# All gate chunks by seven block products, and the retention's heads moved beside the branch products

## The chip, the core and the metric

The kernel runs on one core of a Trainium2 chip. The core has a matrix engine (TensorE, PE in the rows), whose weight loads are shown apart (PEld), an elementwise engine (VectorE, DVE), an engine for activation functions (ScalarE, ACT), a general one (GpSimd, POOL) and SyncE (SP), which here only issues DMAs. Sixteen DMA engines serve them all. The metric is the device time of one launch in microseconds (us).

## The reference

One encoder layer on 256 tokens of width 2048, in float32. Cut to what matters here:

```
h = rmsnorm(x);  proj = h @ w_in            # neighbourhood q,k,v | retention q,k,v,gate | cross-attention q | 3 gates
o_na  = neighbourhood_attention(...)        # 8 heads of 128
o_ret = head_group_norm(retention(fwd) + retention(bwd)) * silu(rg)      # 8 heads, v of 256 a head
o_mem = cross_attention(..., rmsnorm(mem) @ w_mem_kv)                    # 4 heads of 256
merged = sigmoid(g_na) * (o_na @ w_br_na) + sigmoid(g_mem) * (o_mem @ w_br_mem) + sigmoid(g_ret) * (o_ret @ w_br_ret)
x = x + merged @ w_out
x = x + square(relu(rmsnorm(x) @ w_ff1)) @ w_ff2
```

## The kernel before

**Three matmuls for one product.** Every float32 operand is split into a high and a low part: ACT copies the high part (`w_hi`, L95), DVE subtracts it to get the low one (`w_lo`, L96). A product is then hi*hi, lo*hi and hi*lo, three matmuls in `mm3` (L102 to L104).

**Units.** The program is a list of units, which TensorE works through in order. A plain unit multiplies two blocks of 128 rows of a weight (one tile of 512 KB, 128x1024) for both halves of the tokens into 512 columns: 12 matmuls. Eight such units make a chunk of 512 columns of `w_in`; a chunk of `w_br_na` or `w_br_mem` has four. A unit's weights are loaded four units ahead (`issue`, queue SP, five `raw` buffers) and split two units ahead (`do_split`, four buffers each of `w_hi` and `w_lo`).

**Seven block products.** `seven` computes two chunks at once by a scheme of Strassen's kind: 7 instead of 8 block products, each in four units of 6 matmuls (`Product`), so 28 units and 168 matmuls for two chunks where the plain way takes 192. It needs sums of weight blocks. `b1` and `b2` are rings of two buffers each: `ring_load` loads a block into one by SP, `ring_add` adds another block onto it in the DMA itself, issued by POOL (L666), and `do` adds one tile to another on DVE (L682) before the split. A unit's actions have leads: (8, ...) runs eight units ahead of the product, `LEAD` is 14, `L_SPLIT` is 3. For one k the units stand in the order m3, m5, m7 of k-1, m6, m2, m4. In m5 `b1` is the sum of two blocks; in m6 `b1` gets `b2` added on DVE, after which `b2` gets another block added by DMA for m7.

**Order of the stages.** Attention and cross-attention first; then half of the retention's projections; then five pairs of gate chunks by `seven`, with the other 80 plain units of the retention's projections spread between their 140 units; then the last two gate chunks, plainly (`gate_plain`, 16 units); then the branch products with `w_br_na` (16 units), `w_br_mem` (16) and `w_br_ret` (32), whose results are multiplied by the fetched gates on DVE and summed into `merged` (L930, L933, L934); then `w_out`; then the feed-forward layer, whose first product again runs by `seven` in seven pairs (`ff1_pair`) with the plain units of the second product between.

**Tasks.** Smaller work stands in generators that `run_tasks` steps after each unit, at most two steps a unit, at most one that wants the PSUM pool `pt` and one that wants `ps`. `ret_group` fetches what two retention heads need (spilled to DRAM earlier), computes their decay factors, transposes q and k, and spawns the two heads (`ret_head`) and the next group. A head has a chain of products, splits, statistics, a power on POOL (`rsqrt_mean`, L168) and transposes (L554). A scheduler then sorts each engine's instructions by when it holds them to be ready, so the final order is not that of the code.

Of the kernel before, what the change touches and what calls it, by code (L numbers as in the profile page):

```python
# [12 lines left out]
F32 = mybir.dt.float32  # L13
# [44 lines left out]
def encoder_layer(ctx: ExitStack, tc: tile.TileContext, a, out):  # L58
# [259 lines left out]
    def new_T(name):  # L318
        return [quad(f"{name}_{x}") for x in ("hi", "lo")]
# [147 lines left out]
    def decay_factors(g):  # L467

        lg, Fd, V = na_env["lg"], na_env["Fd"], nc.vector
        e1, e2 = cst["dist_f"], cst["dist_b"]  # L470
        Fq = quad("Fd", F32).rearrange("p a s -> p (a s)")
        for h in (2 * g, 2 * g + 1):
            t = t2f("junk")[:, :3 * P]
            Fd[h] = Fq[:, (h % 2) * 3 * P:(h % 2 + 1) * 3 * P]
            V.tensor_scalar_mul(t, e1, lg[:, h:h + 1])
            V.scalar_tensor_tensor(t, e2, lg[:, RET_H + h:RET_H + h + 1], t, op0=ALU.mult, op1=ALU.add)
            nc.scalar.activation(t, t, AF.Exp)
            V.tensor_scalar_mul(Fd[h], t, RET_QK ** -0.5)
# [23 lines left out]
    def ret_group(g):  # L502

        q2 = by_tok(fetch(ret_dram["q", g], "ret_q"))
        v = [by_tok(fetch(d, f"ret_v_{x}", F32R)) for d, x in zip(ret_dram["v", g], ("hi", "lo"))]
        gs = by_tok(fetch(ret_dram["g", g], "ret_gs"))
        yield None, 4
        decay_factors(g)
        T = new_T("ret_qkT")
        for t in range(NT):  # L510
            yield "pt", 1
            pt = transposes(q2[:, t, :], range(4))
            split(T[0][:, :, t * P:(t + 1) * P], T[1][:, :, t * P:(t + 1) * P], pt)
        for j in range(2):
            spawn(ret_head(2 * g + j, j, T, v, gs, env["oT_ret"]))
        if g + 1 < 4:
            spawn(ret_group(g + 1))

    def ret_head(h, j, qkT, v, gs, oT):
        Fd = na_env["Fd"]  # L520
# [137 lines left out]
    def seven(w1, w2, left, halves, r, finish, out_units):  # L658


        V = nc.vector
        e = {}
        NK = 4

        def land(t, src, eng=nc.sync, **kw):
            eng.dma_start(t.rearrange("p (b c) -> p b c", b=2) if len(src.shape) == 3 else t, src, **kw)  # L666

        def raw_load(key, src):
            e[key] = wp.tile([P, UK * CW], F32, name="raw", bufs=5)
            land(e[key], src)  # L670

        def ring_load(n, k, src):
            if not ring:
                open_rings()
            land(ring[n][k % 2], src)

        def ring_add(n, k, src):
            land(ring[n][k % 2], src, nc.gpsimd, accum_op=ALU.add)

        def do(key, raw, add=None):  # L680
            if add is not None:
                V.tensor_tensor(raw, raw, add, op=ALU.add)  # L682
            e[key] = split_w(raw)

        def product(b, form, k, hl, start, stop):
            hi, lo = (by_k(t, halves) for t in hl)
            for j in range(UK):
                mm3(bank[b].rearrange("p (b c) -> p b c", b=2), *left(form, UK * k + j), hi[:, j], lo[:, j],
                    start and j == 0, stop and j == UK - 1)

        def plus(o, b, x, t):

            if r is None:
                V.tensor_tensor(o, bank[b], x, op=ALU.add)
            else:
                V.scalar_tensor_tensor(o, bank[b], r[:, t:t + 1], x, op0=ALU.mult, op1=ALU.add)

        def m1(k):
            def mm():
                if not bank:  # L700
                    open_banks()
                product("X", "A11", k, e.pop(("s1", k)), k == 0, k == NK - 1)
                if k == NK - 1:
                    e["m1"] = t2f("m1")
                    nc.scalar.activation(e["m1"], bank["X"], AF.Copy, **({} if r is None else {"scale": r[:, 0:1]}))
            return Product(mm, [(L_LOAD, lambda: raw_load(("r1", k), w1[k])),
                                (L_SPLIT, lambda: do(("s1", k), e.pop(("r1", k))))])

        def m2(k):
            def mm():  # L710
                product("X", "A12", k, e.pop(("s2", k)), k == 0, k == NK - 1)
                if k == NK - 1:
                    e["c11"] = e["m1"]
                    plus(e["c11"], "X", e["m1"], 0)
            return Product(mm, [(L_LOAD, lambda: raw_load(("r21", k), w1[NK + k])),
                                (L_SPLIT, lambda: do(("s2", k), e[("r21", k)]))])

        def m3(k):
            def mm():
                product("M3", "S4", k, e.pop(("s3", k)), k == 0, k == NK - 1)  # L720
            return Product(mm, [(8, lambda: ring_load("b2", k, w2[NK + k])),
                                (L_SPLIT, lambda: do(("s3", k), ring["b2"][k % 2]))])

        def m5(k):
            def mm():
                product("M5", "S1", k, e.pop(("s5", k)), k == 0, k == NK - 1)
            return Product(mm, [(LEAD, lambda: ring_load("b1", k, w1[k])),
                                (LEAD - 3, lambda: ring_add("b1", k, w2[k])),
                                (L_SPLIT, lambda: do(("s5", k), ring["b1"][k % 2]))])

        def m6(k):
            def pre():
                do(("s6", k), ring["b1"][k % 2], ring["b2"][k % 2])
                ring_add("b2", k, w2[k])

            def mm():
                product("M6", "S2", k, e.pop(("s6", k)), k == 0, k == NK - 1)
                if k == NK - 1:
                    e["u2"] = t2f("u2")
                    V.tensor_tensor(e["u2"], bank["M6"], e["m1"], op=ALU.subtract)  # L740
                    e["c12"] = t2f("c12")
                    V.tensor_tensor(e["c12"], bank["M5"], e["u2"], op=ALU.add)
                    V.tensor_tensor(e["c12"], bank["M3"], e["c12"], op=ALU.add)
            return Product(mm, [(L_SPLIT, pre)])

        def m4(k):
            def mm():
                product("M4", "A22", k, e.pop(("s4", k)), k == 0, k == NK - 1)
            return Product(mm, [(L_SPLIT, lambda: do(("s4", k), ring["b1"][k % 2], e.pop(("r21", k))))])

        def m7(k):
            def mm():
                product("M7", "S3", k, e.pop(("s7", k)), k == 0, k == NK - 1)
                if k == NK - 1:
                    u3 = e["u2"]
                    V.tensor_tensor(u3, u3, bank["M7"], op=ALU.subtract)
                    e["c22"] = t2f("c22")
                    V.tensor_tensor(e["c22"], bank["M5"], u3, op=ALU.add)
                    plus(u3, "M4", u3, 1)
                    e["c21"] = u3  # L760
                    spawn(finish(e))
            return Product(mm, [(L_SPLIT, lambda: do(("s7", k), ring["b2"][k % 2]))])

        out_units += [m1(k) for k in range(NK)]
        for k in range(NK):
            out_units += [m3(k), m5(k)] + ([m7(k - 1)] if k else []) + [m6(k), m2(k), m4(k)]
        out_units.append(m7(NK - 1))
# [56 lines left out]

    gate_dram = {}

    def put_gate(key, sg):
        yield None, 2
        gate_dram[key] = spill(sg, "sg")

    def gate_pair(key, c, ci, to):
        def finish(e):
            sgs = [quad("sg", F32) for _ in range(2)]
# [6 lines left out]
                gate_dram[key, c + i] = spill(sgs[i], f"sg_{key}{c + i}")  # L840

        seven(win(ci), win(ci + 1), x_left, False, r_x, finish, to)

    def gate_plain(key, c, ci):
        def done_gate(acc):
            sg = quad("sg", F32)
            for t in range(NT):
                nc.scalar.activation(by_tok(sg)[:, t, :], acc[t], AF.Sigmoid, scale=r_x[:, t:t + 1])
            spawn(put_gate((key, c), sg))

        chunk(win(ci), hT, KT, done_gate)

    def ret_chunks(g, to):
        def put(key, ts, x=""):
# [39 lines left out]
    ret = ret[16:]  # L894
    sv = []
    for key, c, ci in (("w_br_na", 0, 8), ("w_br_na", 2, 10), ("w_br_mem", 0, 12), ("w_br_mem", 2, 14),
                       ("w_br_ret", 0, 28)):
        gate_pair(key, c, ci, sv)
    n = len(ret)
    for i, x in enumerate(sv):  # L900
# [6 lines left out]
        bank.clear()  # L907

    at(len(units) + 1, end_of_seven)
    at(len(units) + 3, lambda: spawn(ret_group(0)))  # L910
    for i in range(2):
        gate_plain("w_br_ret", 2 + i, 30 + i)


    def branch(wname, oT_key, nkt, first, last):
        at(len(units) - 8, lambda: env[oT_key].back()) if oT_key != "oT_ret" else None
        for c in range(4):
# [25 lines left out]
            at(len(units) - 1, fetch_gate)  # L943
            chunk(w_chunk(wname, c), env[oT_key], nkt, done_br)

    branch("w_br_na", "oT_na", 8, True, False)
    branch("w_br_mem", "oT_mem", 8, False, False)
    branch("w_br_ret", "oT_ret", 16, False, True)
# [145 lines left out]
    for i in range(n_units):  # L1094
# [19 lines left out]
            fn()  # L1114
        do_mm(i)
        units_done.append(i)
        run_tasks(i)
    i = n_units
    while tasks:
        run_tasks(i)  # L1120
# [103 lines left out]
```

## Time and profile before

| | |
|---|---|
| median of 3 runs | 1803.22 us (1802.79 to 1804.96) |
| the profiled execution | 1802.82 us |
| its span in the profile | 1801.1 us |
| TensorE (PE) busy | 1777.3 us, 99% |
| weight loads (PEld) busy | 1467.2 us, 81% |
| DVE busy | 1407.4 us, 78% |
| ACT busy | 1046.3 us, 58% |
| granted TensorE clock | 0.999 of full |

The span runs from the first to the last instruction of the profiled execution; 1.7 us of its time lie outside. Busy time is the union of an engine's instructions. A matmul's end is modelled and overlaps the next one's start, so a busy TensorE can still have lost time: the distance from start to start tells more. Idle time of an engine counts only where TensorE waits for it.

### The profile page before, as it was taken

Reading aid. Unit: us, or ns where it says so; the run is one execution under the profiler, and the core shown is the slowest. Engines: PE = TensorE matmul, PEld = TensorE weight load, DVE = VectorE, ACT = ScalarE, POOL = GpSimd, SP = SyncE. Lnnn points to the kernel's source line nnn. Section 1 sums busy time; section 2 is a strip of 40 time slices with the busy share of each in tenths; the row PEclk is TensorE's granted clock in tenths of the full one; section 3 lists DMA queues with packets and bytes.
Section 4 is the critical chain, followed back from the end, with each engine's and each line's share of the span. In section 5 each row is a group of like instructions: output and inputs, shape, how many; then the busy total and the mean of one; then the engine's idle time right before and its main releaser. Section 6 shows DMA issues by size and latency. Waiting matters only on the chain.

```text
span 1801.1 us, 22755 instructions
## 1 busy us (share of the span) xinstructions
PE 1777.3 (99%) x8130; PEld 1467.2 (81%) x8130; DVE 1407.4 (78%) x1793; ACT 1046.3 (58%) x1313; POOL 148.7 (8%) x176
## 2 busy tenths in 40 slices
PE   8999999999999999999999999998999999999999
PEld 7888888888878888887888888776888888888877
DVE  6777766979888888858875556787898988888874
ACT  7665554656565666654434446855565656666552
POOL 0101000000001000101010000010111111010100
PEclk9999999999999999999999999999999999999999
DMA  9756555899898999987676555787889898979864
GB/s 331 270 204 227 187 175 200 269 300 301 274 302 244 309 289 292 309 303 282 230 255 210 184 185 181 226 237 225 242 254 268 235 270 241 261 227 281 222 187 141
DMA packets 148867, 442.62 MB, mean 246 GB/s; under 512 B 14097, under 2 KB 14609, under 8 KB 148753
## 3 DMA queue, kind: packets, MB, share of 16 engines
q1 hardware_dynamic: 123952, 377.54, 59.3%
q0 software_dynamic: 24512, 62.92, 18.2%
q8 instruction: 64, 1.05, 0.2%
q10 hardware_dynamic: 288, 0.70, 0.1%
q14 instruction: 51, 0.41, 0.1%
HBM read 420.13 MB, written 20.97 MB: 245 GB/s over the span
## 4 chain that ended last, share of the span: by engine, by line
PE 83%; DVE 6%; DMA 5%; ACT 2%; issue 2%; POOL 0%; SPq 0%; DVEq 0%; ACTq 0%; POOLq 0%
PE acc L102 22%; PE acc L103 22%; PE acc L104 22%; PE ps L103 4%; PE ps L104 3%; PE ps L102 3%; DVE w_lo L96 3%; DMA b<-in_w_ff 3%; PE pt L102 2%; PE pt L104 2%; PE pt L103 2%; DMA b<-in_w_in 2%; ACT w_hi L95 1%; DVE b L682 1%; PE pt L315 1%
## 5 line engine op out<-in xcount | busy, mean ns | idle before, releaser
L96 DVE TENSOR_TENSOR w_lo<-raw,w_hi 128x1024 fp32r<-128x1024 f32 (+1 forms) x545 | 660.7, 1220 | 200.1 <-ACT w_hi L95 194.6
L95 ACT ACTIVATE w_hi<-raw 128x1024 fp32r<-128x1024 f32 (+1 forms) x545 | 573.3, 1056 | 372.0 <-PE acc L104 289.0
L95 ACT ACTIVATE w_hi<-b 128x1024 fp32r<-128x1024 f32 x240 | 251.8, 1058 | 258.3 <-PE acc L104 115.7
L96 DVE TENSOR_TENSOR w_lo<-b,w_hi 128x1024 fp32r<-128x1024 f32 x240 | 291.3, 1223 | 112.1 <-ACT w_hi L95 110.1
L102 PE MATMUL acc<-w_hi,hT_hi 128*128 128x512 f32 x744 | 292.2, 393 | 5.7 <-ACT hT_hi L98 5.1
L103 PE MATMUL acc<-w_lo,hT_hi 128*128 128x512 f32 x744 | 291.4, 392 | 0.1
L104 PE MATMUL acc<-w_hi,hT_lo 128*128 128x512 f32 x744 | 290.5, 391 | 0.0
L102 PE MATMUL acc<-w_hi,fT_hi 128*128 128x512 f32 x512 | 201.0, 393 | 2.3 <-DVE x L1046 1.8
L103 PE MATMUL acc<-w_lo,fT_hi 128*128 128x512 f32 x512 | 200.2, 391 | 2.4 <-DVE w_lo L96 2.3
L104 PE MATMUL acc<-w_hi,fT_lo 128*128 128x512 f32 x512 | 199.8, 390 | 0.0
L102 PEld LDWEIGHTS acc<-w_hi,hT_hi 128*128 128x128 f32 x744 | 140.3, 189 | 34.7 <-ACT hT_hi L98 5.1
L103 PEld LDWEIGHTS acc<-w_lo,hT_hi 128*128 128x128 f32 x744 | 140.3, 189 | 30.2 <-DVE w_lo L96 2.5
L104 PEld LDWEIGHTS acc<-w_hi,hT_lo 128*128 128x128 f32 x744 | 140.2, 188 | 29.4
L103 PEld LDWEIGHTS acc<-w_lo,fT_hi 128*128 128x128 f32 x512 | 96.4, 188 | 23.8 <-DVE w_lo L96 4.1
L102 PEld LDWEIGHTS acc<-w_hi,fT_hi 128*128 128x128 f32 x512 | 96.5, 189 | 23.2 <-ACT m L1056 1.5
L104 PEld LDWEIGHTS acc<-w_hi,fT_lo 128*128 128x128 f32 x512 | 96.4, 188 | 20.3
L666 POOL DMA_DIRECT2D b<-in_w_ff x56 | 67.8, 1274 | 540.8 <-DVE w_lo L96 113.7
L103 PE MATMUL pt<-w_lo,f_S_hi 128*128 128x512 f32 x192 | 74.9, 390 | 1.2 <-DVE w_lo L96 1.2
L102 PE MATMUL pt<-w_hi,f_S_hi 128*128 128x512 f32 x192 | 74.8, 390 | 0.3 <-ACT w_hi L95 0.3
L104 PE MATMUL pt<-w_hi,f_S_lo 128*128 128x512 f32 x192 | 74.7, 389 | 0.0
L666 POOL DMA_DIRECT2D b<-in_w_in x40 | 34.8, 917 | 424.6 <-DMA b<-in_w_in 318.3
L682 DVE TENSOR_TENSOR b<-b,raw 128x1024 f32<-128x1024 f32 x48 | 58.7, 1223 | 4.4 <-DMA raw<-in_w_in 3.5
(296 smaller groups left out, 2943.5 us busy)
## 6 DMA issues: line engine op xcount, KB each, us to landing
raw<-in_w_in SPq DMA_DIRECT2D x215, 512.0 KB, 5.7
raw<-in_w_ff SPq DMA_DIRECT2D x200, 512.0 KB, 5.9
b<-in_w_ff SPq DMA_DIRECT2D x56, 512.0 KB, 6.2
b<-in_w_ff POOLq DMA_DIRECT2D x56, 512.0 KB, 8.5
b<-in_w_in SPq DMA_DIRECT2D x40, 512.0 KB, 6.1
b<-in_w_in POOLq DMA_DIRECT2D x40, 512.0 KB, 8.3
raw<-in_w_mem_kv SPq DMA_DIRECT2D x32, 512.0 KB, 3.3
raw<-in_w_br_ret SPq DMA_DIRECT2D x32, 512.0 KB, 3.4
```

The lines of the kernel that those rows point to most:

```text
L95: nc.scalar.activation(hi, src, AF.Copy)
L96: nc.vector.tensor_tensor(lo, src, f(hi), op=ALU.subtract)
L102: nc.tensor.matmul(o, lhsT=lh, rhs=rh, start=start, stop=False)
L103: nc.tensor.matmul(o, lhsT=lh, rhs=rl, start=False, stop=False)
L104: nc.tensor.matmul(o, lhsT=ll, rhs=rh, start=False, stop=stop)
L315: nc.tensor.transpose(pt[:, j, :], src[:, b * P:(b + 1) * P], ident)
L666: eng.dma_start(t.rearrange("p (b c) -> p b c", b=2) if len(src.shape) == 3 else t, src, **kw)
L682: V.tensor_tensor(raw, raw, add, op=ALU.add)
```

## The change

- The last two gate chunks of the retention branch become a sixth pair of `seven`; `gate_plain` and `put_gate` go. The 80 plain units are now spread between 168 units of products.
- In m5 the split of the sum is followed at once by the DVE addition of `b2` and by the DMA addition onto `b2`, which m6 did before, and which stood later; the DMA addition onto `b1` is put one unit later (`LEAD - 4`).
- `ret_group(0)` starts three units ahead of the end of the gates, where it started beside the plain gate chunks; the heads now lie beside the first two branch products. Each group spawns the next one right after its decay factors and not after its heads, so that its fetches go earlier.
- Beside these 32 branch units `run_tasks` makes up to three steps a unit.

```diff
@@ ret_group
-        yield None, 4
+        yield None, 3
         decay_factors(g)
+        if g + 1 < 4:
+            spawn(ret_group(g + 1))
         T = new_T("ret_qkT")
...
             spawn(ret_head(2 * g + j, j, T, v, gs, env["oT_ret"]))
-        if g + 1 < 4:
-            spawn(ret_group(g + 1))
@@ seven
         def m5(k):
+            def pre():
+                do(("s5", k), ring["b1"][k % 2])
+                V.tensor_tensor(ring["b1"][k % 2], ring["b1"][k % 2], ring["b2"][k % 2], op=ALU.add)
+                ring_add("b2", k, w2[k])
+
             def mm():
                 product("M5", "S1", k, e.pop(("s5", k)), k == 0, k == NK - 1)
             return Product(mm, [(LEAD, lambda: ring_load("b1", k, w1[k])),
-                                (LEAD - 3, lambda: ring_add("b1", k, w2[k])),
-                                (L_SPLIT, lambda: do(("s5", k), ring["b1"][k % 2]))])
+                                (LEAD - 4, lambda: ring_add("b1", k, w2[k])),
+                                (L_SPLIT, pre)])
 
         def m6(k):
-            def pre():
-                do(("s6", k), ring["b1"][k % 2], ring["b2"][k % 2])
-                ring_add("b2", k, w2[k])
-
...
-            return Product(mm, [(L_SPLIT, pre)])
+            return Product(mm, [(L_SPLIT, lambda: do(("s6", k), ring["b1"][k % 2]))])
@@ the gates
-                       ("w_br_ret", 0, 28)):
+                       ("w_br_ret", 0, 28), ("w_br_ret", 2, 30)):
         gate_pair(key, c, ci, sv)
...
-    at(len(units) + 3, lambda: spawn(ret_group(0)))
-    for i in range(2):
-        gate_plain("w_br_ret", 2 + i, 30 + i)
+    at(len(units) - 3, lambda: spawn(ret_group(0)))
...
+    u_br = len(units)
     branch("w_br_na", "oT_na", 8, True, False)
@@ the main loop
-        run_tasks(i)
+        run_tasks(i, 3 if u_br <= i < u_br + 32 else 2)
```

How the scheduler's order moves is shown at three places. First DVE in the branch products. Before, this is the stretch in which the two heads of the third group begin, beside the end of the first branch product: `w_lo` is the split of a unit's weights, `pr` and `prT_lo` belong to the heads, `merged` is a gate's multiplication.

```order
L96 TENSOR_TENSOR w_lo_7782<-raw_7725,w_hi_7781 128x1024
L96 TENSOR_TENSOR ret_qkT_lo_7665<-pt_7772,ret_qkT_hi_7664 128x4x128
L96 TENSOR_TENSOR w_lo_7800<-raw_7754,w_hi_7799 128x1024
L96 TENSOR_TENSOR w_lo_7831<-raw_7779,w_hi_7830 128x1024
L930 TENSOR_TENSOR merged_7817<-acc0_7731,sg_7697 128x512
L930 TENSOR_TENSOR merged_7817<-acc1_7732,sg_7697 128x512
L96 TENSOR_TENSOR w_lo_7865<-raw_7797,w_hi_7864 128x1024
L528 TENSOR_TENSOR pr_7855<-ps_7848,Fd_7653 128x256 x2
L96 TENSOR_TENSOR w_lo_7897<-raw_7828,w_hi_7896 128x1024
L96 TENSOR_TENSOR prT_lo_7859<-pr_7855,prT_hi_7858 128x512
```

After the change DVE has this in the second branch product, where the third group's heads end (`z`, `oT_ret2_lo`) while the fourth's begin (`pr`):

```order
L96 TENSOR_TENSOR w_lo_8193<-raw_8085,w_hi_8192 128x1024
L172 TENSOR_TENSOR rs_y_8034<-rs_y0_8032,rs_t_8033 128x2
L99 SCALAR_TENSOR_TENSOR oT_ret2_lo_8111<-pt_8105,c_gains_81,oT_ret2_hi_8110 128x256
L547 TENSOR_SCALAR z_8041<-ps_8012,mv_8026,rs_y_8034 128x256 x2
L919 TENSOR_TENSOR junk_8065<-acc0_7908,sg_7862 128x512
L549 TENSOR_TENSOR z_8041<-z_8041,ret_gs_7403 128x512
L920 TENSOR_TENSOR merged_7320<-merged_7320,junk_8065 128x512
L919 TENSOR_TENSOR junk_8068<-acc1_7909,sg_7862 128x512
L528 TENSOR_TENSOR pr_8078<-ps_8071,Fd_7789 128x256
L920 TENSOR_TENSOR merged_7320<-merged_7320,junk_8068 128x512
L528 TENSOR_TENSOR pr_8078<-ps_8071,Fd_7789 128x256
```

Where five of ten rows were weight splits, one of eleven is: the groups overlap. (Before, such a run without weight splits also stands once in each group.) In the order of TensorE the last transposes of the four groups' second heads stand in units 3, 12, 24 and 32 of the branches before (counted from 0), and in 11, 17, 22 and 27 after; the first transpose of q and k moves from eight units ahead of the branches to unit 1 in them.

Second DVE at the end of the last feed-forward pair, before: `b1_1` is split for m5 of the last k, `b2_0` for m7 of the k ahead of it, and then comes the addition of `b2_1` to `b1_1`.

```order
L96 TENSOR_TENSOR w_lo_14658<-b2_1_10089,w_hi_14657 128x1024
L96 TENSOR_TENSOR w_lo_14668<-b1_1_10087,w_hi_14667 128x1024
L96 TENSOR_TENSOR w_lo_14680<-b2_0_10088,w_hi_14679 128x1024
L682 TENSOR_TENSOR b1_1_10087<-b1_1_10087,b2_1_10089 128x1024
L96 TENSOR_TENSOR w_lo_14706<-raw_14677,w_hi_14705 128x1024
```

And the same place after the change:

```order
L96 TENSOR_TENSOR w_lo_14698<-b2_1_10129,w_hi_14697 128x1024
L96 TENSOR_TENSOR w_lo_14708<-b1_1_10127,w_hi_14707 128x1024
L727 TENSOR_TENSOR b1_1_10127<-b1_1_10127,b2_1_10129 128x1024
L96 TENSOR_TENSOR w_lo_14722<-b2_0_10128,w_hi_14721 128x1024
L96 TENSOR_TENSOR w_lo_14748<-raw_14719,w_hi_14747 128x1024
```

The addition now stands ahead of the split of `b2_0`. Over all pairs it stood one instruction behind m5's split in 29 of 48 places and two to six behind in the others; now it is one behind in 38 of 52 and two in 14. In the first feed-forward pair the last two were adjacent before and are so now.

Third the DMAs that POOL issues at the end of the gates, before: all additions onto `b1` and `b2` (L666) come ahead of the fetches of the retention's v and of the first branch's operand (`oT_na`).

```order
L666 DMA b_1_3366<-in_w_in 128x1024
L666 DMA b_0_3367<-in_w_in 128x1024
L666 DMA b_1_3368<-in_w_in 128x1024
L128 DMA ret_v_hi<-d_ret_v_0_3606 128x1024
L128 DMA ret_v_lo<-d_ret_v_1_3608 128x1024
```

After the change the fetches stand between the last additions:

```order
L666 DMA b_1_3368<-in_w_in 128x1024
L128 DMA oT_na_hi<-d_oT_na_hi 128x1024
L128 DMA oT_na_lo<-d_oT_na_lo 128x1024
L128 DMA oT_na_hi<-d_oT_na_hi 128x1024
L128 DMA oT_na_lo<-d_oT_na_lo 128x1024
L666 DMA b_1_3366<-in_w_in 128x1024
L128 DMA ret_v_hi<-d_ret_v_0_3602 128x1024
L666 DMA b_0_3367<-in_w_in 128x1024
L128 DMA ret_v_lo<-d_ret_v_1_3604 128x1024
L666 DMA b_1_3368<-in_w_in 128x1024
```

Six fetches of 512 KB moved ahead of the last three additions, or among them, in the queue of POOL.

## Rows read from the trace of the kernel before

**Rows 1.** The page: span, two engines' busy time, the chain that ended last.

```profile
span 1801.1 us, 22755 instructions
PE 1777.3 (99%) x8130; PEld 1467.2 (81%) x8130; DVE 1407.4 (78%) x1793; ACT 1046.3 (58%) x1313; POOL 148.7 (8%) x176
...
PE 83%; DVE 6%; DMA 5%; ACT 2%; issue 2%; POOL 0%; SPq 0%; DVEq 0%; ACTq 0%; POOLq 0%
```

**Rows 2.** Timeline of PE at 900 us: start, duration, instruction.

```profile
899.84 0.39 PE L104 MATMUL acc<-w_hi,oT_mem_lo 128*128 128x512 f32 x1
...
901.65 0.39 PE L104 MATMUL acc<-w_hi,oT_mem_lo 128*128 128x512 f32 x1
901.88 0.28 PE L102 MATMUL ps<-ret_qkT_hi 128*128 128x256 f32 x1
...
902.47 0.28 PE L104 MATMUL ps<-ret_qkT_hi,ret_qkT_lo 128*128 128x256 f32 x1
```

**Rows 3.** Waits of PE, whole span: us in total, times, longest.

```profile
PE pt L554 <- DVE ret_qkT_lo L96: 3.6, 3, 1.4
```

**Rows 4.** Windows: gates, first feed-forward pair, end of the last; then the retention.

```profile
core 0: us, PE busy (x) PEld busy (x) DVE busy (x) ACT busy (x) POOL busy (x), PEclk, DMA share, GB/s
354.90:763.10 408.20, 407.82 (x1793) 335.32 (x1792) 347.17 (x341) 250.87 (x265) 38.12 (x47) 1.00 0.93 290
1160.00:1250.00 90.00, 84.10 (x363) 67.40 (x362) 70.85 (x69) 50.82 (x57) 10.04 (x9) 0.98 0.85 245
1690.00:1735.00 45.00, 41.80 (x182) 32.91 (x182) 38.27 (x40) 26.62 (x31) 3.64 (x3) 1.00 0.69 193
785.00:930.00 145.00, 141.43 (x719) 118.79 (x718) 117.70 (x221) 65.52 (x84) 15.36 (x28) 1.00 0.71 255
```

**Rows 5.** Windows 785 to 930 us, by tile: acc, w_lo, sg.

```profile
785.00:930.00 145.00, 123.14 (x511) 1.00 0.71 255
785.00:930.00 145.00, 66.32 (x171) 32.03 (x170) 51.55 (x43) 1.00 0.71 255
785.00:930.00 145.00, 10.44 (x16) 1.38 (x2) 1.00 0.71 255
```

**Rows 6.** DVE's groups from 763 to 940 us: busy, mean ns, idle before.

```profile
L934 DVE TENSOR_TENSOR merged<-merged,junk 128x512 f32<-128x512 f32 x8 | 5.4, 686 | 0.0
...
L169 DVE TENSOR_TENSOR rs_t<-rs_y 128x2 f32<-128x2 f32 x8 | 1.3, 161 | 8.6 <-POOL rs_y L168 8.6
```

**Rows 7.** DMA queues in the gates, 354.9 to 763.1 us: packets, MB, share; issues.

```profile
q1 hardware_dynamic: 25680, 93.53, 61.5%
q0 software_dynamic: 6754, 24.61, 30.9%
...
b<-in_w_in POOLq DMA_DIRECT2D x39, 512.0 KB, 8.1
```

**Rows 8.** Timelines of DVE and PE, end of the last feed-forward pair.

```profile
1704.94 2.35 DVE L96 TENSOR_TENSOR w_lo<-b,w_hi 128x1024 fp32r<-128x1024 f32 x2
1709.99 1.22 DVE L96 TENSOR_TENSOR w_lo<-b,w_hi 128x1024 fp32r<-128x1024 f32 x1 [2.70 <-ACT w_hi L95]
1711.13 1.22 DVE L682 TENSOR_TENSOR b<-b,b 128x1024 f32<-128x1024 f32 x1
...
1726.05 0.50 PE L103 MATMUL acc<-w_lo,fT_hi 128*128 128x512 f32 x1 [1.28 <-DVE w_lo L96]
1730.38 0.50 PE L102 MATMUL acc<-w_hi,fT_hi 128*128 128x512 f32 x1 [0.78 <-DVE x L1046]
```

**Rows 9.** The chain that ended last, same place: start us, us, what.

```profile
1695.56 13.23 DMA b<-in_w_ff
...
1712.89 7.75 DMA b<-in_w_ff
```

**Rows 10.** First feed-forward pair: timeline of DVE, then the chain.

```profile
1210.39 1.23 DVE L682 TENSOR_TENSOR b<-b,b 128x1024 f32<-128x1024 f32 x1
...
1212.62 11.24 DMA b<-in_w_ff
```

More of the change, by code (lines that the diff above doesn't have):

```diff
@@ L825, in encoder_layer @@
     gate_dram = {}
-    def put_gate(key, sg):
-        yield None, 2
-        gate_dram[key] = spill(sg, "sg")
     def gate_pair(key, c, ci, to):
@@ L842, in gate_pair @@
         seven(win(ci), win(ci + 1), x_left, False, r_x, finish, to)
[L844 to L851, printed above, removed]
     def ret_chunks(g, to):
```

## The prediction

> **What bounds the kernel now.** I read the page first, then TensorE's timeline, its waits, and the windows of the stages that change. The page has TensorE busy for 1777.3 of 1801.1 us and on 83% of the chain that ended last [rows 1]. That busy time could hide gaps, since a matmul's shown 0.39 us overlaps the next one, so I measured from start to start: from 899.84 to 901.88 there are nine matmuls of 512 columns, 2.04 us or 0.2267 each; from 901.88 to 902.47 five of 256 columns, 0.118 each [rows 2]. With that price a stage shows what it loses. The gates take 408.20 us; their 140 product units of 6 matmuls and 80 plain units of 12 make 1800, at 0.2267 408.1 (the window holds 1793 of them, 406.5) [rows 4]. So the gates lose 0 to 1.7 us. From 785 to 930 us 719 matmuls and transposes run, 511 of them for chunks [rows 4, 5]: 511 x 0.2267 = 115.8. The other 208 are the retention's: 18 of 256 columns a head, 144 x 0.118 = 17.0, and 64 transposes, which I put at the same 0.11, 7.0. That is 139.8 of 145.0, so the retention costs 5.2 us of waiting, 3.6 of it seen as waits for DVE's `ret_qkT_lo` [rows 3]. The first feed-forward pair (1160 to 1250 us) loses about 8 (363 x 0.2267 = 82.3) and the end of the last one (1690 to 1735) about 4 (182 x 0.2267 = 41.3) [rows 4]. All else is TensorE working without a gap; a matmul less is worth its 0.2267 us wherever no new wait takes its place.
>
> The Trainium skill (Perfetto Trace Analysis, Identifying the Most-Contended Engine) says that the matmul's busy share is no good measure of how full TensorE is, and that the weight loads' share is one; by it the engine is 81% full [rows 1] and could have slack, so that fewer matmuls might bring nothing. The constant 0.2267 us speaks against that here; it is the fifth case below.
>
> **The change part by part.** *Fewer matmuls.* Two plain chunks are 192, a pair by seven products is 168: 24 x 0.2267 = 5.4 us less. The work around them changes by little: 32 weight splits become 36 with 8 additions on DVE, about 14 us more on an engine that is busy 347 of 408 us in the gates [rows 4], where TensorE hides it; without that cover each costs the 1.2 us of a split (51.55 us for 43) [rows 5].
>
> *A denser gate stage.* It becomes 168 x 6 + 80 x 12 = 1968 matmuls, 446.1 us. The DMA engines were busy 0.93 of 408.2 us, 379.6 [rows 4]. A transfer by SP's queue costs 0.615 x 408.2 / (93.53 / 0.524) = 1.41 us, one by POOL's 0.309 x 408.2 / (24.61 / 0.524) = 2.69 [rows 7]. The sixth pair adds 16 loads, 8 additions and 2 spills: 18 x 1.41 + 8 x 2.69 = 46.9. So 426.5 of 446.1, a share of 0.956. On the mean that still fits. But six fetches now stand among the last three additions in POOL's queue, 6 x 1.41 to 6 x 2.69 = 8 to 16 us of DMA in a stage with 4% to spare; what is late then is the last pair's m5, and behind it the splits that ACT holds in order. An addition is issued seven units ahead of its split, 7 x 446.1 / 248 = 12.6 us, and lands in 8.1 [rows 7], so 4.5 us of lateness are free. I take 1 us, with 0 and 6 as the ends (an excess of 8 to 16 less 4.5, of which part lies under the branches that follow).
>
> *Sums sooner.* Where the addition on DVE was adjacent to m5's split nothing moves. In the first feed-forward pair it was: the addition at 1210.39, the DMA at 1212.62 that takes 11.24 us [rows 10]; the loss there stays. At the end of the last pair it was not. DVE had m5's split done by 1707.3, then waited for `b2_0`, which landed at 1708.8 (1695.56 + 13.23) [rows 9], split it at 1709.99 and added at 1711.13 [rows 8]; the DMA at 1712.89 took 7.75 [rows 9], and TensorE waited 1.28 and 0.78 us behind it [rows 8]. In the new order the addition runs at about 1707.3, the DMA some 4 us earlier, and both waits go, with the start-to-start loss around them about 2.4 us. In the gates at most the 1.7 us that they lose can come back; I take 0.6. Sum 3.0, ends 0 (the transfers collide elsewhere) and 4.1 + 3 (the first pair's chain eases too). The addition onto `b1` goes out a unit later, 1.8 us; the 4.5 us above cover it, and without them it would cost those 1.8 a pair.
>
> *The retention beside the branches.* It began eight units ahead of the branches and ended with them, 10 units a group; now it begins in unit 1 and ends in unit 27, and the last three groups follow each other in 5.3 units. DVE's work for the retention is the 117.70 us from 785 to 930 [rows 4] less 51.55 for weight splits, 10.44 for gate products [rows 5] and 5.4 for the sums into `merged` [rows 6]: 50.3, and in each of eight heads it sits waiting for POOL's power, 8.6 in all [rows 6]. So 14.7 us a group. A unit's split is 1.20, the evictions of a chunk of four units 1.3 (first branch) to 2.6. Before, in 10 units: 12.0 + 14.7 + 4 = 30.7 on DVE against 10 x 2.72 + 6.0 = 33.2 on TensorE: covered on the mean, and 5.2 us lost by its bursts. Now, in 5.3 units: 6.4 + 14.7 + 2.8 = 23.9 against 14.4 + 6.0 = 20.4. DVE becomes the bound for three groups, by 3.5 us each, 10.5. Four `w_hi` buffers let splits run three units ahead, 8.2 us, which is used up once. So the added loss lies between 10.5 - 8.2 = 2.3 and 10.5, or near 0 if the third step per unit lets the heads' chains fill each other's waits for POOL (up to 8.6). I take 3: above the lowest, since bursts eat from the same lead. If the lead is gone, the matmuls behind `w_lo` are late, then the accumulators' evictions, then the next chunk. Fetching ahead is free if its queue is: the operand must only be there by unit 1.
>
> *Sum.* -5.4 + 1 - 3.0 + 3 = -4.4 us: the profiled execution's 1802.82 becomes 1798.4. It lies 0.4 under the median of the runs, so I say **1798.8 us**. A measurement of this kernel tells about 0.2%, 3.6 us, from no change.
>
> **The rivals.** *The heads are covered* (chance 0.17): the steps of two groups fill each other's waits, the branch stage loses no more than the old one's 5.2 or even gains 3 of it back, and the sums bring 4 to 7: 1803.2 - 5.4 - 3 - 5 = 1790. For it: 8.6 us of DVE waits for POOL can be filled. Against it: DVE's sum per group is longer than TensorE's even without them (21.7 against 20.4).
>
> *DVE sets the pace of the branches* (0.13, the other side): the whole 10.5 us show, and the bursts of a group wait in turn for TensorE: with the same 5.2 us again, 15.7, the kernel gets slower, -5.4 + 15.7 - 2.4 = +7.9, 1811. It decides from 12 us of added wait on. For it: a stretch of eleven rows on DVE with one weight split. Against: the lead of three units.
>
> *The DMA engines bind in the gates* (0.16): the additions land late once the fetches come among them, 6 us: -5.4 + 6 + 3 - 2.4 = +1.2, 1804. The Trainium skill (DMA: Bandwidth & Descriptors, Issuing engines are not separate DMA queues) says that DMAs of all issuing engines end on the same 16 DMA engines and interleave, so POOL's fetches would slow SP's loads too. The trace agrees so far: with both queues at work the median raw load and the additions share 0.92 of the time (61.5% and 30.9%) [rows 7].
>
> *The change doesn't do what it says* (0.12): the matmuls saved come back as waits for splits, and the sums, adjacent in most places already, bring nothing: 0 + 3 - 2.4, 1803 to 1804.
>
> **How the numbers follow.** My forecast has the chance 0.42, and by itself 1795 to 1802: 2.3 us less to 3 more for the branches, 1 for the rest. The cases give faster by over 0.2% (under 1799.6): 0.30 of the forecast's 0.42, all 0.17 of the covered heads, 0.03 of the rest, 0.50; slower (over 1806.8): 0.11 and 0.03, 0.14; the same: 0.36. The range from 1791.5 to 1806.5 leaves out the lower part of the second case and nearly all of the third, no more than 2 in 10.
>
> **What would show it.** Right: 24 matmuls fewer; the gates at about 446 us with a DMA share near 0.96; DVE nearly without idle time from the tenth branch unit on and TensorE's waits there named `w_lo`, 8 us in all; no wait near the end of the last feed-forward pair. Wrong: TensorE idle inside the gates and ACT waiting there for DMA; or no more wait in the branches than before; or the first feed-forward pair losing other than about 8 us.

## The result, and the profile after

The changed kernel takes **1818.04 us** (median of 5 runs, 1813.13 to 1824.62) where the kernel before, run beside it, takes 1803.22 (5 runs, 1802.79 to 1806.59): 1.0079 of it, 95% interval 1.0055 to 1.0103. It is slower by 0.8%, some 14 us, where 4.4 less were forecast. The kernel before moves a little from chip to chip (medians of 1802.3 to 1805.0), so the experiments below go by ratios, each to the runs of before beside it.

The page of the changed kernel, beside [rows 1]:

```profile
span 1816.3 us, 22804 instructions
...
PE 1779.8 (98%) x8106; PEld 1464.8 (81%) x8106; DVE 1431.3 (79%) x1820; ACT 1059.2 (58%) x1324; POOL 158.3 (9%) x184
...
PE 73%; DMA 11%; DVE 8%; issue 4%; ACT 3%; POOL 0%; SPq 0%; ACTq 0%; DVEq 0%; POOLq 0%
```

The 24 matmuls are gone (8130 to 8106). But DMA's share of the chain that ended last went from 5% to 11%. The windows of the changed stages, columns as in [rows 4]: the gates up to the last pair, the last pair, the branches, 110 us with the first feed-forward pair, the end of the last one.

```profile
361.54:785.00 423.46, 414.40 (x1803) 337.73 (x1802) 361.60 (x351) 261.69 (x273) 39.73 (x47) 1.00 0.93 285
785.00:823.72 38.72, 33.07 (x132) 26.09 (x132) 25.62 (x26) 17.94 (x20) 5.89 (x9) 0.91 0.94 306
823.72:1028.93 205.21, 203.20 (x1002) 169.40 (x1001) 157.15 (x271) 92.20 (x114) 16.09 (x26) 1.00 0.71 248
1175.60:1285.60 110.00, 103.54 (x447) 83.04 (x446) 89.60 (x87) 63.75 (x70) 13.33 (x11) 0.97 0.84 232
1700.00:1755.00 55.00, 54.11 (x242) 44.04 (x241) 46.91 (x47) 33.60 (x38) 3.64 (x3) 1.00 0.78 219
```

At 0.2267 us a matmul the gates lose 423.46 - 1803 x 0.2267 = 14.7 us up to 785 and 38.72 - 132 x 0.2267 = 8.8 in their last pair, 23.5 in all, where they lost at most 1.7 [rows 4]. The branches lose about 4.4 (768 matmuls of 512 columns, 144 of 256 at 0.118 and 88 transposes at 0.11 make 200.8), no more than the 5.2 of before. At the end of the last feed-forward pair next to nothing is lost by this count (242 x 0.2267 = 54.9); measured from start to start it is 1.8 us, where it was 4.8. The first feed-forward pair has 447 matmuls in its 110 us, as the kernel before had in the same stretch of its own. So nearly the whole excess is in the gates: their 23.5, less the 1.7 that they lost before, less 5.4 for the matmuls saved, 1 for the branches and 3 for the end of the feed-forward layer, is 12.4. Some 3 more lie ahead of the gates, at the first loads and at 346 us, which I did not follow up.

**Where it is lost.** In the waits of TensorE and of ACT the old wait for `ret_qkT_lo` [rows 3] is gone. These have grown, from 24.5, 0.3, 3.0 and 1.2 us in the kernel before (whole span; us in total, times, longest):

```profile
ACT w_hi L95 <- DMA b<-in_w_in: 44.6, 13, 6.5
...
PE pt L102 <- ACT w_hi L95: 10.8, 4, 4.6
...
PE acc L103 <- DVE w_lo L96: 5.5, 7, 1.3
...
PE pt L103 <- DVE w_lo L96: 4.4, 7, 0.8
```

The bank `pt` with `w_hi` is a unit of m5 or m7. Here is the end of the first gate pair, timeline of the changed kernel (PE 410.49 is m5 of the last k; DVE 407.70 the sum that has to be done before `b2` may be added to; POOL 411.21 two additions; ACT 422.38 the split for the last m7, PE 423.49 that m7):

```profile
407.70 1.23 DVE L727 TENSOR_TENSOR b<-b,b 128x1024 f32<-128x1024 f32 x1
410.49 0.39 PE L102 MATMUL pt<-w_hi,f_S_hi 128*128 128x512 f32 x1
411.21 1.76 POOL L666 DMA_DIRECT2D b<-in_w_in  x2 [15.96 <-DMA b<-in_w_in]
422.38 1.06 ACT L95 ACTIVATE w_hi<-b 128x1024 fp32r<-128x1024 f32 x1 [5.14 <-DMA b<-in_w_in]
423.49 0.50 PE L102 MATMUL pt<-w_hi,f_S_hi 128*128 128x512 f32 x1 [0.60 <-ACT w_hi L95]
424.75 0.50 PE L103 MATMUL pt<-w_lo,f_S_hi 128*128 128x512 f32 x1 [0.76 <-DVE w_lo L96]
...
427.74 0.50 PE L103 MATMUL acc<-w_lo,hT_hi 128*128 128x512 f32 x1 [1.33 <-DVE w_lo L96]
```

And the same place in the kernel before:

```profile
410.71 1.23 DVE L682 TENSOR_TENSOR b<-b,b 128x1024 f32<-128x1024 f32 x1
412.37 1.75 POOL L666 DMA_DIRECT2D b<-in_w_in  x2 [11.98 <-DMA b<-in_w_in]
413.28 0.39 PE L102 MATMUL pt<-w_hi,f_S_hi 128*128 128x512 f32 x1
...
423.31 1.06 ACT L95 ACTIVATE w_hi<-b 128x1024 fp32r<-128x1024 f32 x1 [1.92 <-DMA b<-in_w_in]
...
428.24 0.39 PE L102 MATMUL pt<-w_hi,f_S_hi 128*128 128x512 f32 x1
```

The transfer is equally late in both: DMA at about 412, landed at about 423. What changed is how soon it is wanted. From m5 to the last m7 there were 15.0 us of TensorE's work (five product units and three plain ones, 5 x 1.36 + 3 x 2.72); now there are five and two, 12.2 us. With that ACT sits 5.14 us, all splits behind it wait, and TensorE meets them as `pt` and then as `acc`. The sum is ready at 408.93, but POOL sends the addition only at 411.79: its queue holds the next pair's first addition onto `b1` ahead of it, which waits for its load. Both then share the DMA engines. The chain that ended last has this addition; the load at 774.24 and the addition at 789.26 in the last gate pair; and the addition at the end of the first feed-forward pair (start us, us, what):

```profile
411.79 10.48 DMA b<-in_w_in
...
774.24 13.38 DMA b<-in_w_in
...
789.26 14.74 DMA b<-in_w_in
...
1230.43 14.31 DMA b<-in_w_ff
```

In the last gate pair no next pair stands in the queue, and it is not the pair's last addition that is late but the one before it, for m7 of the last k but one. Fetches stand around it. Timelines of DVE (the sum that this addition waits for) and of POOL there, and TensorE's longest wait:

```profile
779.00 1.23 DVE L727 TENSOR_TENSOR b<-b,b 128x1024 f32<-128x1024 f32 x1
...
788.16 0.88 POOL L666 DMA_DIRECT2D b<-in_w_in  x1 [18.80 <-DMA b<-in_w_in]
788.72 0.88 POOL L128 DMA_DIRECT2D ret_v_hi<-d_ret_v  x1
789.26 1.23 POOL L666 DMA_DIRECT2D b<-in_w_in  x1
...
805.21 0.79 PE L102 MATMUL pt<-w_hi,f_S_hi 128*128 128x512 f32 x1 [4.65 <-ACT w_hi L95]
...
807.06 0.63 PE L104 MATMUL pt<-w_hi,f_S_lo 128*128 128x512 f32 x1
807.49 0.63 PE L102 MATMUL pt<-w_hi,f_S_hi 128*128 128x512 f32 x1
```

The sum is done at 780.23, yet the addition onto `b2` leaves at 789.26, 9 us later. In POOL's queue it stands behind the same pair's addition onto `b1` (788.16), and that one waits for its load by SP, which is sent at 774.24 and takes 13.38 us while the four fetches of `oT_na` are under way. So the queue is at work here too; the fetches make the load in front late, and then the transfer of the addition itself (14.74 us).

So the theory to test, **Q**: at a pair's end the addition onto `b2` is late by its place in POOL's queue and by what shares the DMA engines with it, and the thinner plain units no longer cover that. Rivals: **S**, the new order of the sums makes the waits; **T**, the DMA engines are simply full; **F**, the fetches among the last additions make them.

One part of the change does nothing: with `LEAD - 3` put back in place of `LEAD - 4` in the changed kernel, the scheduled program has the same order of instructions on all five engines, row for row (buffer numbers aside). So the unit in which that addition is written doesn't set its place here.

### The profile page after: what moved, and what is told of

Its sections match the earlier page's. It is cut to its first block, busy times and chain, and to the rows that moved or that the text cites. A ratio compares the mean times of both kernels' runs of the same rounds, so it can differ in the third digit from the quotient of the medians.

```text
span 1816.3 us, 22804 instructions
## 1 busy us (share of the span) xinstructions
PE 1779.8 (98%) x8106; PEld 1464.8 (81%) x8106; DVE 1431.3 (79%) x1820; ACT 1059.2 (58%) x1324; POOL 158.3 (9%) x184
## 4 chain that ended last, share of the span: by engine, by line
PE 73%; DMA 11%; DVE 8%; issue 4%; ACT 3%; POOL 0%; SPq 0%; ACTq 0%; DVEq 0%; POOLq 0%
PE acc L103 19%; PE acc L104 19%; PE acc L102 19%; DMA b<-in_w_in 7%; DVE w_lo L96 5%; PE ps L103 3%; PE ps L102 3%; PE ps L104 3%; DMA b<-in_w_ff 2%; ACT w_hi L95 2%; PE pt L103 2%; PE pt L104 2%; PE pt L102 2%; DMA raw<-in_w_in 1%; PE pt L315 1%
## 5 line engine op out<-in xcount | busy, mean ns | idle before, releaser
L96 DVE TENSOR_TENSOR w_lo<-raw,w_hi 128x1024 fp32r<-128x1024 f32 (+1 forms) x537 | 649.7, 1219 | 179.4 <-ACT w_hi L95 174.3
L95 ACT ACTIVATE w_hi<-b 128x1024 fp32r<-128x1024 f32 x260 | 273.1, 1059 | 268.2 <-PE acc L104 137.7
L96 DVE TENSOR_TENSOR w_lo<-b,w_hi 128x1024 fp32r<-128x1024 f32 x260 | 315.3, 1222 | 136.7 <-ACT w_hi L95 134.5
L102 PE MATMUL acc<-w_hi,hT_hi 128*128 128x512 f32 x688 | 270.8, 395 | 6.8 <-ACT hT_hi L98 4.9
L103 PE MATMUL acc<-w_lo,hT_hi 128*128 128x512 f32 x688 | 270.7, 394 | 4.0 <-DVE w_lo L96 3.9
L104 PE MATMUL acc<-w_hi,hT_lo 128*128 128x512 f32 x688 | 269.5, 392 | 0.0
L102 PEld LDWEIGHTS acc<-w_hi,hT_hi 128*128 128x128 f32 x688 | 130.6, 190 | 34.0 <-ACT hT_hi L98 4.9
L103 PEld LDWEIGHTS acc<-w_lo,hT_hi 128*128 128x128 f32 x688 | 130.2, 189 | 34.1 <-DVE w_lo L96 8.0
L104 PEld LDWEIGHTS acc<-w_hi,hT_lo 128*128 128x128 f32 x688 | 130.1, 189 | 27.1
L666 POOL DMA_DIRECT2D b<-in_w_ff x56 | 68.1, 1363 | 535.2 <-DMA b<-in_w_ff 173.8
L666 POOL DMA_DIRECT2D b<-in_w_in x48 | 42.4, 959 | 473.0 <-DMA b<-in_w_in 383.8
L727 DVE TENSOR_TENSOR b<-b,b 128x1024 f32<-128x1024 f32 x52 | 63.6, 1223 | 1.3
```

The source lines that it names most:

```text
L95: nc.scalar.activation(hi, src, AF.Copy)
L96: nc.vector.tensor_tensor(lo, src, f(hi), op=ALU.subtract)
L102: nc.tensor.matmul(o, lhsT=lh, rhs=rh, start=start, stop=False)
L103: nc.tensor.matmul(o, lhsT=lh, rhs=rl, start=False, stop=False)
L104: nc.tensor.matmul(o, lhsT=ll, rhs=rh, start=False, stop=stop)
L727: V.tensor_tensor(ring["b1"][k % 2], ring["b1"][k % 2], ring["b2"][k % 2], op=ALU.add)
```

## The experiments

**1. The changed kernel with the old order of the sums.**

```
@@ m5
...
-                V.tensor_tensor(ring["b1"][k % 2], ring["b1"][k % 2], ring["b2"][k % 2], op=ALU.add)
-                ring_add("b2", k, w2[k])
...
-                                (LEAD - 4, lambda: ring_add("b1", k, w2[k])),
+                                (LEAD - 3, lambda: ring_add("b1", k, w2[k])),
...
@@ m6
+                do(("s6", k), ring["b1"][k % 2], ring["b2"][k % 2])
+                ring_add("b2", k, w2[k])
...
```

> The changed kernel with the old order of the sums (m6 adds b2 and sends the addition onto b2, b1 at LEAD - 3), all else as changed. Theory Q (the chain at each pair's end: the addition onto b2 stands behind the next pair's addition onto b1 in POOL's queue, and fewer plain units lie between the split of m5 and that of m7 to hide it): the waits at the pairs' ends stay, 12 to 16 us of them in the gates, so 1815 to 1821 us. Theory S (the new order of the sums makes the waits): they go, about 14 us less than the changed kernel, 1804 us. By both the end of the last feed-forward pair loses its 3 us again.

Measured 1825.83 us, 1.0120 of before [1.0105 to 1.0135]. S falls: without the new order the kernel is slower still, by 0.4% or 7 us. Q had the sign, but the time lies above its range (1815 to 1821), since it took the new order for worth 3 us.

**2. The kernel before with the new order of the sums alone.**

```
@@ m5
...
+                V.tensor_tensor(ring["b1"][k % 2], ring["b1"][k % 2], ring["b2"][k % 2], op=ALU.add)
+                ring_add("b2", k, w2[k])
...
@@ m6
-                do(("s6", k), ring["b1"][k % 2], ring["b2"][k % 2])
-                ring_add("b2", k, w2[k])
...
+            return Product(mm, [(L_SPLIT, lambda: do(("s6", k), ring["b1"][k % 2]))])
```

> The kernel before with only the new order of the sums (five pairs, plain last chunks, heads where they were). Theory Q: 80 plain units over 140 product units still hide the chain, no waits at the pairs' ends, 3 us gained at the end of the last feed-forward pair: about 1800 us. Theory S: waits of 2 to 4 us at the ends of the five gate pairs, 1811 to 1816 us.

Measured 1798.33 us, 0.9967 [0.9955 to 0.9980], 6.0 us faster. Its gates, window:

```profile
363.00:809.10 446.10, 446.10 (x1990) 369.82 (x1989) 371.01 (x372) 277.29 (x288) 38.15 (x48) 1.00 0.92 294
```

TensorE is busy in all of it, so with three plain units beside each pair's end there is no wait. Start to start, the gates win 2 us and the feed-forward layer 4; in the latter's first pair 10 us are still lost, as before.

**3. The order in POOL's queue.** One dependence without a semaphore (`NOSYNC`) puts a pair's last addition onto `b2` ahead of the next pair's first one onto `b1`.

```
@@ ring_add, where i is its DMA
+            if n == "b2":
+                last_b2[0] = i
+            elif k == 0 and last_b2[0] is not None:
+                tc.add_manual_dep(i.ins, last_b2[0].ins.name, NOSYNC)
```

> The changed kernel with one order turned round in POOL's queue: the last addition onto b2 of a pair goes out ahead of the next pair's first addition onto b1. Theory Q: at the ends of the first five gate pairs the split of m7 no longer waits, 10 to 14 us less in the gates, and part of the first feed-forward pair's 10.7 us goes too; the 8 us at the end of the last gate pair, where the fetches stand, stay: 1800 to 1808 us. Theory S, or a theory by which the DMA engines are simply full there (T): no change beyond 3 us, 1815 to 1821.

Measured 1799.26 us, 0.9966 [0.9955 to 0.9976]: 19 us less than the changed kernel, by an order of two DMAs, and just under Q's range. The first gate pair's end (timeline), then the answer of the DMA view for this addition:

```profile
409.86 0.86 POOL L679 DMA_DIRECT2D b<-in_w_in  x1 [12.11 <-DVE b L733]
...
412.32 0.86 POOL L679 DMA_DIRECT2D b<-in_w_in  x1 [1.59 <-DMA b<-in_w_in]
...
418.04 1.06 ACT L95 ACTIVATE w_hi<-b 128x1024 fp32r<-128x1024 f32 x1 [0.30 <-PE acc L104]
...
423.23 0.39 PE L102 MATMUL pt<-w_hi,f_S_hi 128*128 128x512 f32 x1
```

```profile
b<-in_w_in POOLq DMA_DIRECT2D x1, 512.0 KB, 7.4
```

It leaves 1.9 us sooner and lands in 7.4 us in place of 10.5, and ACT waits for TensorE instead of for it. S and T fall for these ends. The waits at the first five ends are gone, and the loss in the first feed-forward pair falls from 10.7 us, start to start, to 3.4: much of it was the same queue. The last gate pair still loses 8.6: there the addition in front is the pair's own, and this edit leaves the two as they were.

**4. The first retention group four units later.**

```
-    at(len(units) - 3, lambda: spawn(ret_group(0)))
+    at(len(units) + 1, lambda: spawn(ret_group(0)))
```

> The changed kernel with the first retention group started four units later, so that the fetches of its v leave the last additions in POOL's queue (those of oT_na stay). Theory F (the fetches among the last additions make the waits): the 9 us lost between 790 and 806 us go, 1809 us, and the first five pairs' ends keep theirs. Theory Q: the last pair's end keeps the 2 to 4 us that the others lose, so 5 to 7 us less, 1811 to 1813, less what the heads lose by starting later.

Measured 1819.49 us, 1.0087 [1.0069 to 1.0105], no better than the changed kernel. The last pair's end (785 to 812 us, 27.0 us for 98 matmuls) loses 4.8 in place of 8.8, and the branches lose 2.9 more than in the changed kernel. The time lies above the ranges of both theories. F explains about half of the last pair, by the fetches of v alone (those of `oT_na` stay), and nothing of the other five.

**5. The plain units put where the cover is missing**, POOL's order at the first five ends as in the changed kernel.

```
-        for _ in range((i + 1) * n // len(sv) - i * n // len(sv)):
+        weight = lambda j: sum(2 if x % 28 >= 20 else 1 for x in range(j))
+        for _ in range(weight(i + 1) * n // weight(len(sv)) - weight(i) * n // weight(len(sv))):
```

> The changed kernel with the same 80 plain units put twice as densely beside the last eight product units of each pair as beside the others; POOL's order at the ends of the pairs hardly changes. Theory Q says that two things make the wait there, the place in POOL's queue and too little work of TensorE between the split of m5 and that of m7. If the second counts, the five product units there now last about 17 us in place of 13.3 and the waits at the first five pairs' ends go, 10 to 14 us less: 1804 to 1809 us, unless the additions inside the pairs come late in their turn. If only the queue counts, 1815 to 1821.

Measured 1808.48 us (1802.76 to 1813.32), 1.0031 [1.0018 to 1.0043], about 9 us less than the changed kernel. In the first pair m5 and the last m7 are 19.3 us apart (1.3 of it another wait, for DVE's `ret_gs`), POOL still sends the two additions together (407.11), and no ACT wait is left at that end. So the cover counts too, with the queue as it was. But the gates still lose 16 us (454.30 - 1932 x 0.2267), in pieces of up to 1.8 us, most of them inside the pairs, where the plain units now are rarer: cover was moved, not made, as far as the places tell.

**6. The retention's move alone**, on top of experiment 2 (plain last chunks).

```
@@ ret_group
...
+        if g + 1 < 4:
+            spawn(ret_group(g + 1))
         T = new_T("ret_qkT")
@@ behind gate_plain
-    at(len(units) + 3, lambda: spawn(ret_group(0)))
+    at(len(units) - 3, lambda: spawn(ret_group(0)))
@@ the main loop
+        run_tasks(i, 3 if u_br <= i < u_br + 32 else 2)
```

> The kernel before with the new order of the sums and with the retention's heads moved (started three units ahead of the branches, the next group spawned after the decay factors, three steps a unit), the last two gate chunks plain. Against the same without the move (1798.3 us). The prediction's term (DVE sets the pace): 3 us slower, 1801. Rival (the overlapping heads fill each other's waits): 1 to 2 us faster, 1797.

Measured 1797.61 us, 0.9967 [0.9954 to 0.9979], against 0.9967 without the move. The move costs nothing that can be measured; start to start the branches lose 3.9 us where they lost 5.2.

**7. The fetches behind the gates' last addition**, on top of experiment 3.

```
@@ fetch, where i is its DMA
+        if dt != F32 and last_b2[0] is not None:
+            tc.add_manual_dep(i.ins, last_b2[0].ins.name, NOSYNC)
...
```

> The kernel with the addition onto b2 ahead (1799.3 us, 8.6 us lost at the end of the last gate pair) and with POOL's fetches of oT_na and ret_v put behind the gates' last addition in its queue. Theory F2 (those fetches share the DMA engines with the last additions and make them late): the 8.6 us there go, and 0 to 4 us come back at the start of the branches, whose operand now lands just in time: 1791 to 1795 us. Rival (the last pair's end is late for another reason, its density or SP's loads of the branch weights): 1797 to 1801.

Measured 1795.37 us, 0.9952 [0.9939 to 0.9966]. The gates, then the first 28.6 us of the branches:

```profile
362.00:801.40 439.40, 439.29 (x1934) 362.13 (x1933) 387.16 (x376) 280.80 (x292) 45.34 (x56) 1.00 0.95 294
...
801.40:830.00 28.60, 23.28 (x100) 19.19 (x99) 19.52 (x30) 13.32 (x18) 1.59 (x3) 0.88 1.06 410
```

F2 holds for the gates: six pairs that lose 1.4 us in all, 439.40 us for 1932 matmuls (438.0), at a DMA share of 0.95. The load in front of the last pair's late addition now lands in 7.9 us in place of 13.4, and the addition leaves 3.0 us behind its sum in place of 9. But 7 us come back in the branches, more than the 0 to 4 expected, so that the time lies just above F2's range. There the DMA engines are full (1.06: transfers count where they start), and TensorE waits 5.3 us for the second group's q (the chain):

```profile
809.83 14.18 DMA ret_q<-d_ret_q
...
824.15 1.09 PE pt L319 x4
```

**8. As 7, with the first group four units later** (`len(units) + 1` as in 4).

> As the last, and the first retention group starts four units later, so that SP's fetches of its q and gate go later too. If these two fetches matter for the last additions, 1 to 2 us less than the last kernel; if not, the heads start late and the branches lose 2 to 4 us more: 1794 to 1798 us.

Measured 1799.42 us, 0.9982 [0.9972 to 0.9992]: slower than 7. The branches lose 14.0 us, start to start, in place of 11.5: there the loads of `w_br_na` take up to 16.44 us (chain), and the heads, started later, hold TensorE at their `z` for 3.6 us. The time lies above the stated range.

**9. As 7, with the second group's transposes three units later** (`yield None, 6 if g == 1 else 3`).

> The kernel with the addition onto b2 ahead and the fetches behind the gates' last addition (1795.4 us), where TensorE waits 5.3 us at 818 us for the second retention group's q, which SP issued at 809.83 and which took 14.18 us; here the second group's transposes come three branch units (about 8 us) later. If that fetch is late by itself, those 5 us go: 1789 to 1791.5 us. Rival (the later heads press on DVE or on the last product with w_br_ret): 1793 to 1797.

Measured 1794.26 us, 0.9948 [0.9936 to 0.9961], not to be told from 7. It is the rival's range: the wait for q is gone, and one for a head's statistics stands in its place (waits), in branches that still lose 9 us (window):

```profile
PE pt L558 <- DVE rs_t L173: 3.4, 1, 3.4
```

```profile
801.00:1011.30 210.30, 205.00 (x1002) 170.65 (x1001) 157.18 (x271) 92.46 (x114) 16.40 (x26) 0.99 0.72 258
```

**10. Five pairs with the order of experiment 3**: the kernel before, the new sums, the queue's order.

> The kernel before with the new order of the sums (1798.3 us) and with the addition onto b2 ahead in POOL's queue; five pairs, plain last gate chunks, heads where they were. Theory Q: nothing to gain in its gates, which lose nothing; but in the feed-forward layer the first pair's end, where 6 to 7 us are lost behind the same queue, comes free: 1792 to 1794. If the first feed-forward pair's loss has another cause: 1797 to 1799.

Measured **1792.25 us**, 0.9930 [0.9917 to 0.9944], 12.6 us faster than before. The median lies under that of every kernel with six pairs; the nearest, experiment 9 on the same chip, is 2.0 us higher, and the two intervals just touch. As Q says, the gates stay at no loss, and the first feed-forward pair's falls from 10.1 in experiment 2 to 4.9.

**11. As 10, with the retention's move.**

> Five pairs, the new order of the sums, the addition onto b2 ahead, and the retention's heads moved beside the branches (the last kernel, 1792.3 us, with the move). If the move is worth the 0.7 us that it brought without the queue's change: 1791.5. If the heads now lose more than the 4.4 us that they lose where they were: 1793 to 1795.

Measured 1791.92 us, 0.9937 [0.9925 to 0.9949], not to be told from 10. Its branches hold the same 1002 matmuls as those of 9, in 5 us less:

```profile
805.30:1010.40 205.10, 203.50 (x1002) 169.62 (x1001) 150.84 (x259) 89.50 (x108) 15.16 (x26) 1.00 0.67 237
```

## Why the prediction was wrong

**A denser gate stage** is the step that failed: +1 us forecast, ends 0 and 6, about +22 found. Its sentence "An addition is issued seven units ahead of its split, 7 x 446.1 / 248 = 12.6 us, and lands in 8.1" took one mean for all additions. The additions onto `b2` have less: they can go only after the sum. At the first pair's end the sum is done at 408.93 and ACT is free for the split at 417.24 (422.38 - 5.14), 8.3 us later and not 12.6; the addition stands 2.9 us behind another in POOL's queue and lands in 10.5 us, not 8.1, so it is 5 us late. The step counted how much the DMA engines move, and that count was right (share 0.95 in 7, next to no wait); the latency of one chain and the order in the queue were not looked at. The Trainium skill (DMA: Bandwidth & Descriptors, Issuing engines are not separate DMA queues) says that DMAs of all issuing engines interleave on the same 16 engines; the trace agrees, with 13.4 us for SP's load at 774.24 beside POOL's four fetches and 7.9 where they go later (experiment 7). The rival that used it ("The DMA engines bind in the gates", 1804) had the place and the sign, but only the fetches as a cause, which bear on one pair of six.

The price could have been read before. From m5 to the last m7 TensorE starts 15.0 us apart in the old gates, without loss; 12.7 in the first feed-forward pair, where 3.9 us are lost right behind that m7 (of 10.7 in 110 us, start to start; another 4 follow a wait at 1237, which the chain leads back to a `raw` load); 17.7 in the five pairs after it, without loss there. Here are the first feed-forward pair's m5 and last m7, PE's timeline of the kernel before:

```profile
1212.38 0.39 PE L102 MATMUL pt<-w_hi,f_S_hi 128*128 128x512 f32 x1
...
1225.07 0.51 PE L102 MATMUL pt<-w_hi,f_S_hi 128*128 128x512 f32 x1 [0.28 <-ACT w_hi L95]
```

So the chain needs about 15 us, and at times more: the change took the gates to 12.2 in four of six pairs and left 15.0 in two. Of the four, three lost 2.3 to 4.4 us at this place, and the last pair lost its 8.8 one k sooner; the two with 15.0 lost 2.2 and 0.3 us.

**Fewer matmuls**, -5.4: right in the gates (experiment 7), and still not a gain. The work beside them was counted too low: two plain chunks are 16 units with a split each and a pair is 28, so 16 splits become 28, and not 32 become 36. With the 8 additions that is 20 instructions of about 1.2 us more on DVE, 24 us and not 14; the pages have 23.9 more (1407.4 to 1431.3). In the gates TensorE hid it (experiment 7). The plain chunks had also been the place where the operands of the branches came in. With six pairs those fetches either meet the last additions (3) or fill the DMA engines under the first branch units (7 to 9), and the branches give back 5 us (9 against 11, whose branches hold as many matmuls).

**Sums sooner**, -3.0 with ends 0 and -7.1: right in mechanism, too small; -6.0 alone, and about -7 in the changed kernel. The gates gave 2 where I took 0.6, the feed-forward layer 4 where I took 2.4. That the first feed-forward pair's 8 us would stay held for the change. That the addition onto `b1` goes out a unit later was no cost, since it doesn't.

**The retention beside the branches**, +3 with ends 0 and 10.5: the lower end, 0 (experiment 6). From the tenth unit on DVE was nearly without idle time, as forecast (46.04 of 50 us), but TensorE hardly waited for it (once for `z`, 1.6 us, and never for `w_lo` in the branches):

```profile
855.00:905.00 50.00, 48.06 (x263) 40.27 (x263) 46.04 (x111) 22.65 (x33) 9.34 (x15) 1.00 0.62 218
```

```profile
L169 DVE TENSOR_TENSOR rs_t<-rs_y 128x2 f32<-128x2 f32 x8 | 1.3, 161 | 3.5 <-POOL rs_y L168 3.5
```

The second row is DVE's group that waits for POOL's power: 3.5 us where it was 8.6 [rows 6]. The overlapping heads fill each other's waits, as the rival "The heads are covered" had it; the 14.7 us that I put for a group held 2.2 of such waits. Of what was to show it wrong, "TensorE idle inside the gates and ACT waiting there for DMA" came true, and so did "no more wait in the branches than before" (4.4 us against 5.2).

## What to carry to other kernels

Ask of each transfer on a cyclic chain how long the chain is and how much of the bound engine's work lies between its two ends; a mean lead and a mean landing time hide the one that is short, and a near miss (ACT waiting 1.9 us, TensorE not) tells that little is left. Work taken out of a schedule is also cover taken out: count what was hidden behind it. And before a stage is given more, look at the order in the queue that feeds it; here turning round two DMAs was worth more than 24 matmuls.

## What the runs showed of the hardware

After the 4.65 us wait at 805 us the granted clock of TensorE was 0.50 between 805 and 810 us, the lower of its two levels (1.2 GHz), and ten matmuls started 0.42 to 0.43 us apart (807.06, 807.49) in place of 0.2267. That adds 2 us to the wait. Experiments 3 and 7 show the same behind waits of 4.6 and 5.3 us (12 and 9 such matmuls). So here a wait of 5 us cost about 7. Shorter waits differ: behind 0.60 and 0.76 us at 423 us the granted clock stayed at 1.00 (423 to 428 us); behind 1.06 and 0.76 us at 656 us it was 0.50 from 658 to 661; and in the kernel before, behind 2.14 us at 1240 us, it was 0.50 from 1240 to 1243.

A DMA that POOL has to send waits for those ahead of it in POOL's queue: of two additions, the one whose sum was ready at 780.23 us left at 789.26, 1.1 us behind the one whose load landed at 787.62. With the order of two such additions turned round (experiment 3) the later one left with its own sum, 1.9 us sooner.
